# A fourteenth seven-product pair in each half of a down projection, and three kept sums reused across the halves

## Chip, core and metric

The kernel runs on one core of a Trainium2 chip. The metric is device time in microseconds; the median of three runs before the change is 1292.85 us (1292.70 to 1292.91). The engines are TensorE (PE; its weight loads are PEld), VectorE (DVE), ScalarE (ACT), GpSimd (POOL) and SyncE (SP). In this kernel SP issues the loads of weights, and POOL issues, in this stage, the reads of sums that were kept in DRAM.

## What is computed

One layer of an encoder over 256 positions of width 2048, in float32. The change touches the last product, `act @ w_down`, with an inner dimension of 5504 = 43 x 128.

```
def conv_ffn(x, g_norm, w_up, conv_k, conv_b, w_down):
    h = rms_norm(x, g_norm)
    up = h @ w_up
    ...
    gate, val = jnp.split(up, 2, axis=-1)
    return x + (jax.nn.silu(gate) * val) @ w_down
```

A final RMSNorm follows. Everything before (a mixer block with two branches, an output projection, the up projection) is as it was.

## The kernel before

**Precision.** Each float32 operand is kept as a high and a low part, and a product is three matmuls (`triple`, L315 to L320: high by high, low by high, high by low). ScalarE makes the high part of a weight piece (L171), VectorE the low part by a subtraction (L172).

**Tiling of the down projection.** The 2048 output columns are done in two halves of 1024 (`g_dn`, two `wide` groups run by `run_wide`). Within a half the 43 inner chunks come as 21 pairs and a single one. A *piece* is one chunk's weights, 128 x 1024, 512 KB, so a half has pieces 0 to 42, and the second half's follow on. The pair that comes q-th is said to stand at *place* q; its pieces are 2q and 2q + 1.

**Two kinds of pairs.** A plain pair takes 2 pieces x 4 result blocks x 3 = 24 matmuls. A seven-product pair uses Winograd's form of the 2 x 2 block product (positions 2 x 128, chunks 2, columns 2 x 512): seven block products of three matmuls, 21 in all. Its first step (piece 2q) has three products, nine matmuls: blocks of the activations by blocks of both pieces' weights, the third with a sum of activations; its second step (piece 2q + 1) has four, twelve matmuls, with sums of weights in the order u13, u13, u24, u24. It accumulates in four banks P beside the four of the result, C. `ev_sums` adds the P banks into the result after the last such pair (a first half of five VectorE operations, L993 to L998, a second of three), `ev_down` and `finish` evict C.

**The sums.** The activation sums of each seven-product pair are made in the up projection (`sums`, `sums_split` in `ev_up`; four operations on 128 x 128 blocks and a split) and written to DRAM; in the down projection `stored` reads them back on POOL's queue, 512 KB, into one of three tiles s0, s1, s2 in turn, in both halves. The weight sums are of two kinds. For most pairs they are made on the spot: four VectorE additions of 128 x 512 (`weight_sums`, L361 to L365) in tiles t13 and t24, then split by ScalarE (L375) and VectorE (L376) into h13, l13, h24, l24, one tile each. For the pairs of DOWN_SPLIT (6, 10, 14, 18) they are made in the up projection (`split_ahead`), kept in DRAM as down_h and down_l, and read by `split_read` (four reads of 512 KB on POOL) into another set of tiles, one each. In a seven-product pair the first piece is split in its first half only; for a pair of DOWN_SPLIT only that half is loaded.

**Order.** The order of instructions on each engine is that of the program, written by hand. `begin(i)` precedes piece i's matmuls: it issues loads up to piece i + 4, splits piece i + 3, then runs the tasks listed for i, in the order in which they were listed. `wide` lists its tasks when the work is planned: for a pair whose first piece is i, the read of its activation sums at i - 4, weight sums at i - 3, their split at i - 2; for a pair of DOWN_SPLIT all reads at i - 6. Others are listed while the program runs: the convolution, gate and split of an up group at 1, 2 and 3 pieces behind its end (L1066 evicts it, L1072 to L1079 convolve), `ev_sums` at 1 and 2 behind the last seven-product pair. Raw weights have five buffers (`wraw`), split ones four (`whi`, `wlo`).

`down_order` lays the kept pairs (DOWN_PAIRS) on the places of DOWN_QUADS[g] and the others, in rising order, on the places left. The last four pieces of the second half are done block by block.

Of the kernel before, what the change touches and what calls it, by code (L numbers as in the profile page):

```python
# [25 lines left out]
NF = DFF // 128  # L26
# [42 lines left out]
TURN_X2 = (13, 1)  # L69
Y_GAP = 224  # L70
PAD = 16
DOWN_PAIRS = (3, 5, 6, 7, 9, 10, 11, 13, 14, 15, 17, 18, 19)
DOWN_QUADS = (DOWN_PAIRS, (2, 4, 5, 6, 8, 9, 10, 12, 13, 14, 16, 17, 18))
DOWN_SPLIT = (6, 10, 14, 18)
DOWN_JOBS = ((1, 3), (5, 7), (9, 11), (13, 17))
FIN_AT = 36
# [3 lines left out]
def trunk_kernel(ctx, tc, x, x_t, vecs, w_in, ln_g, ln_b, w_st, b_s, rpb, w_branch, w_out, w_up, w_down,  # L80
# [204 lines left out]
    def wide(src, row0, order, c0, acts, quads, room, done, sums=None, stored=None, split=None, late=False, lead=4, behind=()):  # L285
        n0 = plan_wide(src, row0, order, c0)
        boxes = {}
        for q in quads:
            i = n0 + 2 * q
            k = order[2 * q]  # L290
            units[i], units[i + 1] = 1, 2
            b = boxes[q] = {}
            ready = split[0].get(k // 2) if split else None
            if stored:
                b["acts"] = {}
                at(i - (ready[0] if ready else lead), lambda b=b, k=k: stored(k // 2, b["acts"]))
            else:
                b["acts"] = sums[k]
            if ready:
                halved.add(i)  # L300
                for n, lead in zip(("13", "24"), ready[-2:]):
                    at(i - lead, lambda b=b, k=k, n=n: split[1](k // 2, b, n))
                continue
            whole[i] = whole[i + 1] = None
            halves = late and q == quads[0]
            at(i - 3, lambda i=i, b=b, halves=halves: weight_sums(i, b, room, halves))
            if halves:
                at(i - 2, lambda b=b: b.pop("rest")())
            at(i - (1 if q in behind else 2), lambda b=b: weight_sums_split(b, room))
        return ("wide", n0, order, acts, quads, boxes, done)  # L310
# [41 lines left out]
    def sums_of(o):  # L352
        return [(o[:, 0, n * 128:(n + 1) * 128], o[:, 1, n * 128:(n + 1) * 128]) for n in range(4)]
# [629 lines left out]
    def ev_sums(j, room):  # L983
        def done(P, i):
            x2 = rs["x2"]
            p1, p5, p6, p7 = P
            x11, x12, x21, x22 = (x2[:, t, c * 512:(c + 1) * 512] for t in range(2) for c in (j, j + 1))
            m = {}

            def first_half():  # L990
                ab, cd = room("t13", F32), room("t24", F32)
                m["v"], m["u3"], m["w"] = cd[:, 0], cd[:, 1], ab[:, 0]
                nc.scalar.activation(ab[:, 0], p1, AF.Copy)  # L993
                nc.vector.tensor_add(x11, p1, x11)
                nc.vector.tensor_sub(ab[:, 1], ab[:, 0], p6)
                nc.vector.tensor_add(m["v"], p5, ab[:, 1])
                nc.vector.tensor_add(m["u3"], p7, ab[:, 1])
                nc.vector.tensor_add(m["w"], p5, m["u3"])  # L998

            def second_half():  # L1000
                nc.vector.tensor_sub(x12, x12, m["v"])
                nc.vector.tensor_add(x21, x21, m["u3"])
                nc.vector.tensor_sub(x22, x22, m["w"])

            at(i + 1, first_half)
            at(i + 2, second_half)
        return done
# [243 lines left out]
    def split_read(kept, g, tile_of, queue=nc.gpsimd):  # L1251
        def read(pair, box, n):
            u = box.setdefault("u", [])
            u.append([tile_of(pair, p + n) for p in "hl"])
            for t, src in zip(u[-1], kept[pair, g][n]):
                queue.dma_start(t.bitcast(F32), src)
            if len(u) == 2:
                split_sums(box, u)
        return read
# [130 lines left out]
    def down_room(name, dt):  # L1390
        return hpool.tile([128, 2, 512], dt, name=h_room[name])

    def stored(pair, box):
        n = ff["turn"] = (ff.get("turn", -1) + 1) % 3
        o = ff["twice"].tile([128, 2, 512], F32R, name="s2") if n == 2 else down_room(f"s{n}", F32R)
        nc.gpsimd.dma_start(o.bitcast(F32), ff["kept"][pair])
        box["s"] = sums_of(o)

    def down_split_tile(pair, name):
        return ff["twice"].tile([128, 2, 512], F32R, name=name)  # L1400
# [1 line left out]
    d_kept = {}  # L1402

    def down_order(g):
        free = [p for p in range(NF // 2) if p not in DOWN_PAIRS]
        kept = list(DOWN_PAIRS)
        pairs = [(kept if q in DOWN_QUADS[g] else free).pop(0) for q in range(NF // 2)]
        return tuple(2 * p + kk for p in pairs for kk in range(2)) + (NF - 1,)

    g_dn = [wide(w_d, 0, down_order(g), g * 1024, lambda k: ff["a"][k], DOWN_QUADS[g], down_room,  # L1410
                 (ev_sums(2 * g, down_room), ev_down if g == 0 else finish), stored=stored,
                 split=({p: (6, 6) for p in DOWN_SPLIT}, split_read(d_kept, g, down_split_tile))) for g in range(2)]
    ff["kept"] = {p: dram.tile([128, 2, 512], F32, name=f"sums{p}") for p in DOWN_PAIRS}
    for p, turn in zip(DOWN_SPLIT, DOWN_JOBS):
# [184 lines left out]
```

## Time and profile before

| | us |
|---|---|
| median of three runs | 1292.85 |
| profiled execution | 1293.06 |
| its span, first to last instruction | 1291.3 |
| down projection within the span | 1066.1 to 1283.2 |

The granted TensorE clock of this execution is 0.998. Rows of the profile are read so: a row of grouped instructions has line, engine, operation, output and inputs, shapes, count, then busy time and mean duration, then the idle time ahead of them and what ended it. A row of the timeline has start, duration, engine, line, operation and tiles; a run of equal instructions is one row with its count; the idle time of the engine ahead of it, and what ended that, stand in brackets. A row of waits has who waited for whom, the total in us, how often, and the longest. A row of a window has its limits, its length, and each engine's busy time (number of instructions), clock, share of the DMA engines and GB/s; asked for VectorE alone it has that engine's only. A row of DMA issues has the number, the size and the median us from issue to landing. A matmul's row overlaps the next one's, so that distances between starts count, not durations.

### The profile page before, as it was taken

To read this page: it belongs to the slowest core of one execution; us is meant where nothing else is said; L and a number is where in the kernel's file an instruction comes from. 1 tells how busy PE (TensorE), PEld (TensorE's weight loads), DVE (VectorE), ACT (ScalarE), POOL (GpSimd) and SP (SyncE) were. 2 spreads that over 40 slices of the span, in tenths; PEclk is the share of its full clock that TensorE was granted. 3 is DMA by queue.
4 is the path that set the end of the run, shared out by engine and by line. 5 is a ranking of instruction groups with operands and counts; after the bars stand their busy time and mean duration, and the time that the engine had idled before them with its cause. 6 is when DMAs were issued, how large, how long until landed. Compare 5 with 4: busy or idle time off the path is not lost.

```text
span 1291.3 us, 19690 instructions
## 1 busy us (share of the span) xinstructions
PE 1281.6 (99%) x6653; PEld 1092.7 (85%) x6653; DVE 1143.6 (89%) x1712; ACT 815.7 (63%) x1229; POOL 174.5 (14%) x309
## 2 busy tenths in 40 slices
PE   9999999999999999999999999999999999999997
PEld 7888888888888888888888888888888888888885
DVE  7898978888889988996888899998988989989987
ACT  7776577877855655566566656566665656555554
POOL 0003706334000001100001001100000001211210
PEclk9999999999999999999999999999999999999999
DMA  9779879998799977965588788888877859998993
GB/s 368 273 272 282 289 236 306 322 316 300 275 335 349 353 244 244 412 225 164 182 295 274 239 297 290 270 267 285 266 220 222 279 171 363 368 388 325 353 383 146
DMA packets 199893, 369.51 MB, mean 286 GB/s; under 512 B 15984, under 2 KB 124144, under 8 KB 199792
## 3 DMA queue, kind: packets, MB, share of 16 engines
q1 hardware_dynamic: 175472, 286.36, 64.6%
q0 software_dynamic: 23888, 81.23, 17.8%
q8 instruction: 52, 0.85, 0.3%
q10 hardware_dynamic: 432, 0.66, 0.1%
q14 instruction: 49, 0.40, 0.1%
HBM read 320.48 MB, written 45.61 MB: 284 GB/s over the span
## 4 chain that ended last, share of the span: by engine, by line
PE 98%; DVE 1%; issue 0%; DVEq 0%; ACT 0%; ACTq 0%
PE bank L223 31%; PE bank L227 16%; PE bank L320 12%; PE bank L318 12%; PE bank L319 12%; PE bank L251 5%; PE bank L253 5%; PE bank L252 5%; PE bank L835 1%; DVE wlo L172 0%; PE bank L885 0%; PE bank L499 0%; PE bank L699 0%; PE bank L875 0%; PE bank L973 0%
## 5 line engine op out<-in xcount | busy, mean ns | idle before, releaser
L172 DVE TENSOR_TENSOR wlo<-wraw,whi 128x1024 fp32r<-128x1024 f32 (+1 forms) x472 | 537.0, 1151 | 98.2 <-ACT whi L171 64.2
L171 ACT ACTIVATE whi<-wraw 128x1024 fp32r<-128x1024 f32 (+1 forms) x472 | 463.3, 995 | 187.9 <-PE bank L319 72.4
L223 PE MATMUL bank<-h,whi 128*128 128x512 f32 x1760 | 425.5, 392 | 0.0
L223 PEld LDWEIGHTS bank<-h,whi 128*128 128x128 f32 x1760 | 322.0, 188 | 61.8
L227 PEld LDWEIGHTS bank<-h,wlo 128*128 128x128 f32 x1760 | 225.9, 191 | 8.8
L227 PE MATMUL bank<-h,wlo 128*128 128x256 f32 x1760 | 228.6, 283 | 0.0
L1074 ACT ACTIVATE tc<-ta,ck 128x256 f32<-128x256 f32 x86 | 47.1, 595 | 110.0 <-DVE ta L1072 110.0
L320 PE MATMUL bank<-wlo,a 128*128 128x512 f32 x188 | 73.4, 390 | 0.2 <-DVE wlo L172 0.2
L318 PE MATMUL bank<-whi,h 128*128 128x512 f32 x186 | 73.2, 394 | 0.0
L318 PE MATMUL bank<-whi,a 128*128 128x512 f32 x188 | 73.2, 389 | 0.0
L319 PE MATMUL bank<-whi,a 128*128 128x512 f32 x188 | 73.1, 389 | 0.0
L319 PE MATMUL bank<-whi,h 128*128 128x512 f32 x186 | 72.8, 391 | 0.0
L320 PE MATMUL bank<-wlo,h 128*128 128x512 f32 x186 | 72.6, 390 | 0.0
L1077 DVE SCALAR_TENSOR_TENSOR tc<-ta,ck,tc 128x255 f32<-128x255 f32 x86 | 41.4, 481 | 14.4 <-ACT tc L1074 14.4
L800 POOL TENSOR_SCALAR_AFFINE_SELECT bias<-run 64x128 f32<-64x128 f32 x64 | 39.7, 654 | 85.4 <-DVE sc L843 84.7
L1306 POOL DMA_DIRECT2D down_h<-so x16 | 8.7, 545 | 311.1 <-ACT tc L1084 170.3
L251 PE MATMUL bank<-whi,y 128*128 128x512 f32 x128 | 50.6, 395 | 0.0
L251 PE MATMUL bank<-whi,h 128*128 128x512 f32 x128 | 50.4, 394 | 0.0
L253 PE MATMUL bank<-wlo,h 128*128 128x512 f32 x128 | 49.9, 390 | 0.0
L253 PE MATMUL bank<-wlo,y 128*128 128x512 f32 x128 | 49.9, 390 | 0.0
L252 PE MATMUL bank<-whi,y 128*128 128x512 f32 x128 | 49.8, 389 | 0.0
L252 PE MATMUL bank<-whi,h 128*128 128x512 f32 x128 | 49.8, 389 | 0.0
(332 smaller groups left out, 2075.7 us busy)
## 6 DMA issues: line engine op xcount, KB each, us to landing
wraw<-in_w_up_dram SPq DMA_DIRECT2D x336, 256.0 KB, 4.0
wraw<-in_w_in_dram SPq DMA_DIRECT2D x107, 512.0 KB, 6.3
wraw<-in_w_down_dram SPq DMA_DIRECT2D x78, 512.0 KB, 7.3
wraw<-in_w_in_dram SPq DMA_DIRECT2D x70, 256.0 KB, 6.0
wraw<-in_w_branch_dram SPq DMA_DIRECT2D x32, 512.0 KB, 5.7
wraw<-in_w_out_dram SPq DMA_DIRECT2D x28, 512.0 KB, 6.1
h<-sums POOLq DMA_DIRECT2D x18, 512.0 KB, 7.6
tw<-in_w_down_dram POOLq DMA_DIRECT2D x8, 1024.0 KB, 8.3
```

The costliest lines, as they stand in the source:

```text
L171: nc.scalar.activation(h[:, k, :m], w[:, k, :m], AF.Copy)
L172: nc.vector.tensor_sub(l[:, k, :m], w[:, k, :m], h[:, k, :m].bitcast(F32))
L223: nc.tensor.matmul(p, h[:, k - k0, b * 128:(b + 1) * 128], acts(k), start=k == 0, stop=k == nk - 1)
L227: nc.tensor.matmul(p[:, :T], l[:, k - k0, b * 128:(b + 1) * 128], acts(k)[:, 0, :], start=False, stop=False)
L251: nc.tensor.matmul(p, xh, h[:, kk, :m], start=st, stop=False)
L252: nc.tensor.matmul(p, xl, h[:, kk, :m], start=False, stop=False)
L253: nc.tensor.matmul(p, xh, l[:, kk, :m], start=False, stop=sp)
L318: nc.tensor.matmul(p, xh, h, start=st, stop=False, **kw)
L319: nc.tensor.matmul(p, xl, h, start=False, stop=False, **kw)
L320: nc.tensor.matmul(p, xh, l, start=False, stop=sp, **kw)
L1074: nc.scalar.activation(v, u, AF.Identity, scale=ck[:, 1, ch:ch + 1], bias=ck[:, 3, ch:ch + 1])
L1077: nc.vector.scalar_tensor_tensor(v[:, 1:], u[:, :T - 1], ck[:, 0, ch:ch + 1], v[:, 1:], op0=OP.mult, op1=OP.add)
```

## The change

DOWN_PAIRS becomes the union of two lists, DOWN_KEPT, one for each half, which now also fix the order of the kept pairs. Both lists hold the thirteen pairs of before and pair 2, so each half has 14 seven-product pairs and 7 plain ones, and pair 2's sums are kept too. `stored` remembers which pair stands in which of the three tiles and reads nothing if the pair is already there; the last three kept pairs of the first half (17, 18, 19) are the first three of the second.

Places and kept pairs (an s marks a pair of DOWN_SPLIT, with weight sums from DRAM):

| half | before: pair at place | after: pair at place |
|---|---|---|
| first | 3 at 3; 5, 6s, 7 at 5 to 7; 9, 10s, 11 at 9 to 11; 13, 14s, 15 at 13 to 15; 17, 18s, 19 at 17 to 19 | 2 at 2; 3, 6s, 5 at 4 to 6; 7, 10s, 9 at 8 to 10; 11, 13 at 12, 13; 14s, 15, 17, 18s, 19 at 15 to 19 |
| second | 3 at 2; 5, 6s, 7 at 4 to 6; 9, 10s, 11 at 8 to 10; 13, 14s, 15 at 12 to 14; 17, 18s, 19 at 16 to 18 | 17, 18s, 19 at 1 to 3; 2, 6s, 3 at 5 to 7; 5, 10s, 7 at 9 to 11; 9, 11 at 13, 14; 14s, 13, 15 at 16 to 18 |

```diff
-DOWN_PAIRS = (3, 5, 6, 7, 9, 10, 11, 13, 14, 15, 17, 18, 19)
-DOWN_QUADS = (DOWN_PAIRS, (2, 4, 5, 6, 8, 9, 10, 12, 13, 14, 16, 17, 18))
+DOWN_KEPT = ((2, 3, 6, 5, 7, 10, 9, 11, 13, 14, 15, 17, 18, 19), (17, 18, 19, 2, 6, 3, 5, 10, 7, 9, 11, 14, 13, 15))
+DOWN_PAIRS = tuple(sorted(set(DOWN_KEPT[0] + DOWN_KEPT[1])))
+DOWN_QUADS = ((2, 4, 5, 6, 8, 9, 10, 12, 13, 15, 16, 17, 18, 19), (1, 2, 3, 5, 6, 7, 9, 10, 11, 13, 14, 16, 17, 18))
...
+    down_held = {}
+
     def stored(pair, box):
+        held = [s for p, s in down_held.values() if p == pair]
+        if held:
+            box["s"] = held[0]
+            return
         n = ff["turn"] = (ff.get("turn", -1) + 1) % 3
         o = ff["twice"].tile([128, 2, 512], F32R, name="s2") if n == 2 else down_room(f"s{n}", F32R)
         nc.gpsimd.dma_start(o.bitcast(F32), ff["kept"][pair])
         box["s"] = sums_of(o)
+        down_held[n] = pair, box["s"]
...
     def down_order(g):
-        free = [p for p in range(NF // 2) if p not in DOWN_PAIRS]
-        kept = list(DOWN_PAIRS)
+        free = [p for p in range(NF // 2) if p not in DOWN_KEPT[g]]
+        kept = list(DOWN_KEPT[g])
```

## The prediction

> **What bounds the kernel now.** I read the page first, then the waits of TensorE, then the busy time of the stage that the change touches, the down projection, which runs from 1066.1 us to 1283.2 us of the span.
>
> ```profile
> span 1291.3 us, 19690 instructions
> PE 1281.6 (99%) x6653; PEld 1092.7 (85%) x6653; DVE 1143.6 (89%) x1712; ACT 815.7 (63%) x1229; POOL 174.5 (14%) x309
> PE 98%; DVE 1%; issue 0%; DVEq 0%; ACT 0%; ACTq 0%
> ```
>
> TensorE has no free time, and the chain of work that ended last is 98% TensorE. In the window from 1060 us to the end, its waits by the profile are one line, and VectorE is nearly as full:
>
> ```profile
> PE bank L320 <- DVE wlo L172: 0.2, 1, 0.2
> ...
> 1066.10:1283.20 217.10, 198.09 (x250) 1.00 0.89 335
> ...
> 400.00:800.00 400.00, 400.00 (x2078) 343.39 (x2077) 357.12 (x540) 241.56 (x348) 25.79 (x45) 1.00 0.80 273
> ```
>
> So a matmul removed is time saved only while VectorE (198.09 of 217.10 us busy here, 19.0 idle) and the transfers still deliver each operand in time. Where they are just in time today, anything put ahead of them is a stall of TensorE, and stalls cannot be won back, since nothing behind them is idle.
>
> **The matmuls removed.** A plain pair is 24 matmuls, a seven-product pair 21; one pair changes kind in each half, so six go.
>
> ```profile
> 1077.17 0.39 PE L318 MATMUL bank<-whi,a 128*128 128x512 f32 x1
> 1078.31 0.39 PE L320 MATMUL bank<-wlo,a 128*128 128x512 f32 x1
> ...
> 1273.92 0.39 PE L319 MATMUL bank<-whi,a 128*128 128x512 f32 x1
> 1274.54 0.50 PE L320 MATMUL bank<-wlo,a 128*128 128x512 f32 x1 [0.23 <-DVE wlo L172]
> ```
>
> 1077.17 is the first matmul of piece 4 of the first half; by the loops the one at 1273.92 is the 868th after it, so one matmul takes 196.75 / 868 = 0.227 us. Six are 1.36 us; a plain pair is 5.45 us, a seven-product pair 4.77 us (its first step 2.04, its second 2.72). **Term 1: -1.36 us.**
>
> **The opening of the first half.** The first seven-product pair moves from place 3 (piece 6) to place 2 (piece 4), while VectorE still does the convolution of the last up group.
>
> ```profile
> 1071.67 2.35 DVE L172 TENSOR_TENSOR wlo<-wraw,whi 128x1024 fp32r<-128x1024 f32 x2
> 1073.94 0.75 DVE L1072 TENSOR_TENSOR ta<-ta,rb 128x256 f32<-128x256 f32 x2
> ...
> 1076.86 1.22 DVE L172 TENSOR_TENSOR wlo<-wraw,whi 128x1024 fp32r<-128x1024 f32 x1
> ...
> 1078.33 0.68 DVE L172 TENSOR_TENSOR wlo<-wraw,whi 128x512 fp32r<-128x512 f32 x1
> 1078.93 0.68 DVE L364 TENSOR_TENSOR h<-wraw 128x512 f32<-128x512 f32 x1
> ...
> 1081.46 0.42 DVE L543 TENSOR_TENSOR a<-tc,a 128x256 fp32r<-128x256 f32 x1
> ```
>
> The first row splits pieces 3 and 4 (2.27 us from start to next start, 1.135 each), the convolution takes 1073.94 to 1076.86 = 2.92, then piece 5 is split. A half split costs 0.60 (1078.33 to 1078.93), the four weight sums 2.53 (1078.93 to 1081.46). In the changed kernel begin(1) splits half of piece 4 and then makes the weight sums of pieces 4 and 5; that task was listed when the work was planned, the convolution only when its group ended, so the sums go first; the rows 1078.93 to 1081.46 show that order, as L543 too was listed late and stands behind the sums of the same begin. Piece 5's split starts at 1071.67 + 1.135 + 0.60 + 2.53 + 2.92 = 1078.86 and ends 1.22 later, 1080.08. TensorE needs its low half in the sixth matmul of the pair, which is where the row 1078.31 stands; with the 0.05 us that the wait at 1274.54 shows behind the end of its split (1273.27 + 1.22, below) it goes on at 1080.13. Nothing covers this: VectorE is busy all the way. **Term 2: +1.8 us** (1.5 to 2.1). The sums' own splits follow at 1081.2 and 1082.4, before TensorE, now late, wants them (1081.5 and 1082.9).
>
> **The read of pair 18 in the first half.** Pairs 6, 10, 14 and 18 get their weight sums from DRAM, into one set of tiles. From pair 14 to pair 18 there were four places (14 to 18), one pair between them plain; now there are three (15 to 18), all seven-product.
>
> ```profile
> 1243.55 0.39 PE L320 MATMUL bank<-l,h 128*128 128x512 f32 x1
> ...
> 1244.24 0.53 POOL L1396 DMA_DIRECT2D h<-sums  x1 [4.22 <-PE bank L320]
> ...
> 1246.32 0.53 POOL L1256 DMA_DIRECT2D l<-down_l  x1
> ...
> l<-down_l POOLq DMA_DIRECT2D x1, 512.0 KB, 13.0
> ...
> l<-down_l POOLq DMA_DIRECT2D x1, 512.0 KB, 15.2
> ...
> DMA to landing us min/median/max: 7.6/11.5/15.2
> ```
>
> Five reads leave in a row once the earlier pair's sums have been used: 0.69 us after the ninth matmul of its second step began (1243.55 to 1244.24), the fifth 2.08 us after the first. So the fifth leaves 8 x 0.227 + 0.69 + 2.08 = 4.59 us after that second step began. It is needed in the ninth matmul of pair 18's second step. From second step to second step there lie 12 + 21 + 21 + 9 = 63 matmuls, 14.30 us; with 1.82 that is 16.12, so the read has 11.5 us, against 17.0 before. Issue to landing of the fifth read took 13.0 us and 15.2 in the two bursts shown, and 15.2 is the longest of all sixteen l reads: 1.5 to 3.7 too long. Against that, the new order holds VectorE up just there (next term), so fewer weight loads share the transfer engines with the burst; by that the stall could be nothing. **Term 3: +0.9 us**, between nothing and the nearest row's 1.5, closer to the row; ends 0 and 3.7. For this queue the Trainium skill ("DMA: Bandwidth & Descriptors", Anatomy of one DMA) fits 2.0 us plus bytes / 436 GB/s; five reads of 512 KB would by my estimate from it be down in about 8 us, term 3 would be nothing and the sum +1.5. The rows of 13.0 and 15.2 disagree with that where the weights' queue runs too; the same page (Queues, rings and completion order) has the transfer engines take turns between queues, and by my estimate its 6 us of data doubled, and 2.0, give 14.
>
> **Two computed pairs in a row.** Before, a pair with sums from DRAM or a plain one stood between any two whose sums are made here. Now places 12 and 13, 16 and 17 of the first half, 13 and 14, 17 and 18 of the second hold such pairs in a row, and their split sums (h13, l13, h24, l24) have one tile each. ScalarE can write h24 of the second only after the last matmul of the first.
>
> ```profile
> 1097.35 0.39 PE L320 MATMUL bank<-h,a 128*128 128x512 f32 x1
> 1097.76 1.06 ACT L375 ACTIVATE h<-h 128x1024 fp32r<-128x1024 f32 x1 [0.24 <-PE bank L320]
> 1263.22 2.35 DVE L376 TENSOR_TENSOR h<-h,h 128x1024 fp32r<-128x1024 f32 x2
> 1264.17 0.39 PE L318 MATMUL bank<-whi,a 128*128 128x512 f32 x1
> 1265.49 4.62 DVE L172 TENSOR_TENSOR wlo<-wraw,whi 128x1024 fp32r<-128x1024 f32 x4
> 1270.03 0.68 DVE L994 TENSOR_TENSOR x<-bank,x 128x512 f32<-128x512 f32 x1
> ...
> 1273.27 1.22 DVE L172 TENSOR_TENSOR wlo<-wraw,whi 128x1024 fp32r<-128x1024 f32 x1
> ```
>
> ScalarE starts 0.41 us after that matmul's start (1097.35 to 1097.76), so 0.18 after the second pair's first; it takes 1.06, VectorE's l24 another 1.135: l24 is done 2.4 us into the second pair, and is needed 2.04 + 8 x 0.227 = 3.9 us into it. That holds at three of the four, and the pieces split behind it are in time by about 1 us. The fourth is the last pair of the second half, and behind it VectorE has no slack. Today pair 18's matmuls there begin at 1264.17 and VectorE is through the sums' split at 1265.49, 1.32 us later; then come four splits, the first sums of the result (1270.03 to 1273.27) and the split of the last piece, whose product ran at 1274.54 instead of 1273.92 + 0.227 = 1274.15. That chain has no gap. With 2.4 in place of 1.32 it moves 1.1 us later and TensorE with it. **Term 4: +1.1 us** (0.7 to 1.4).
>
> **What is covered.** Pair 2's kept sums add four small and one 128x512 operation on VectorE in the up projection, some 1.8 us by the next rows, plus a write of 512 KB. They fall in the fourth up group, inside 400 to 800 us, where TensorE shows 400.00 of 400.00 us while pairs 6 and 10 already do the same beside such a job: nothing, and at most those 1.8 us.
>
> ```profile
> 1050.66 0.28 DVE L324 TENSOR_TENSOR sw<-tc 128x128 f32<-128x128 f32 x1
> ...
> 1053.91 0.68 DVE L543 TENSOR_TENSOR so<-sw,so 128x512 fp32r<-128x512 f32 x1
> ```
>
> Pair 2's read becomes the first of POOL's queue in this stage, and pair 3's follows.
>
> ```profile
> 1065.63 0.54 POOL L1396 DMA_DIRECT2D h<-sums  x1 [9.95 <-PE bank L227]
> 1066.56 0.54 POOL L1396 DMA_DIRECT2D h<-sums  x1 [0.40 <-PE bank L223]
> ...
> h<-sums POOLq DMA_DIRECT2D x18, 512.0 KB, 7.6
> ```
>
> They leave when the tiles of the up projection are free, at 1065.63 and 1066.56, and 7.6 us later, at 1073.2 and 1074.2, are there; the first is needed at 1077.17 + 6 x 0.227 = 1078.5. Nothing. The reads of kept sums go from 26 to 25 (14 + 11), since pairs 17, 18 and 19 stay in their tiles; no read before was waited for by TensorE, so this gives no time. VectorE's work grows, per half, by 0.60 + 1.135 + 2.53 + 2.27 less a plain pair's 2.27, 4.3 us, so 8.5 of its 19.0 idle us.
>
> **The sum.** -1.36 + 1.8 + 0.9 + 1.1 = +2.4. On the profiled execution (1293.06 us: the span 1291.3 and 1.76 around it) that is 1295.5; the median, 1292.85, lies 0.2 lower, so 1295.3.
>
> **Rivals.** *A, not slower: the opening is covered.* If piece 5 is split ahead of the convolution and the sums, VectorE is done with it by 1076.0 and term 2 is gone. It decides in one place: whether that split ends before 1078.3. Then -1.36 + 1.1 + 0 to 0.9: 1292.6 to 1293.5. For it: ScalarE, which makes the high half first, is busy 63% of the span. Against it: VectorE's order in the rows from 1071.67 on, which has no gap.
>
> *B, clearly slower: VectorE runs out across the two halves.* From the split of piece 32 to that of the second half's piece 3 it has the pairs 15, 17 and 19 at 6.54 us (0.60 + 1.135 + 2.53 + 2.27), 1.74 for pair 18, five plain pieces at 1.135, the result's sums at 3.24 (1270.03 to 1273.27) and 1.81 (1171.65 to 1173.46), the four evictions at 2.4, and 0.60 + 2.53 + 1.135 for pair 17 of the second half.
>
> ```profile
> 1171.65 0.68 DVE L1001 TENSOR_TENSOR x<-x,h 128x512 f32<-128x512 f32 x1
> ...
> 1173.46 1.22 DVE L172 TENSOR_TENSOR wlo<-wraw,whi 128x1024 fp32r<-128x1024 f32 x1
> 1174.60 2.47 DVE L1112 TENSOR_TENSOR x<-bank,x 128x512 f32<-128x512 f32 x4
> ...
> DVE h L365 <- DMA wraw<-in_w_down_dram: 3.5, 6, 1.2
> ```
>
> That is 38.8 us. TensorE's 182 matmuls from piece 29 to where that last split is needed take 41.3, and about 0.8 pass before the first split can start (0.18 and ScalarE's half split): 1.7 to spare, less some 0.7 for the wait for tiles at place 17. Late weights cost VectorE 3.5 us in six waits today, up to 1.2 each; more than one of those here makes a stall. With 1 to 3 us from this or from term 3 at its far end the time is 1296.5 to 1298.5. For it: the transfer engines are 89% busy over the stage. Against: term 3's own stall gives VectorE time.
>
> *C, the reuse doesn't act* and pairs 17, 18 and 19 are read again. Each read takes 7.6 us and would leave when its tile is free, two or more places ahead of its use; TensorE waits for none of this kind today, so this is within 0.3 us of the forecast.
>
> **Chances.** Forecast 0.60 (1293.7 to 1296.5: the terms' bounds, term 3 up to 1.5), A 0.17, B 0.20, C 0.03. A measurement of this kernel can tell about 0.2%, 2.6 us, from no change: up to 1295.4. Of the forecast and C a little over half lie below that, all of B above: slower 0.50, same 0.48. Faster by 0.2% would need 2.6 us; all that six matmuls and the 0.4 at 1274.54 hold is 1.8, so 0.02. The range takes A's upper part and B's lower: 1293.0 to 1298.2.
>
> **What would show it.** TensorE's count falls by 6; L364 runs 20 times in the stage, not 18; 25 reads of sums. Term 2: a wait of L320 on L172 of 1.8 us near 1078. Term 3: a wait on the reads of down_l or down_h near 1162. Term 4: the wait near 1275 grows from 0.2 to about 1.3. The forecast is wrong if TensorE's waits in the stage sum to under 2 us or to more than 6, or if a wait stands at the second half's first pairs.

## The result, and the profile after

| | before | after |
|---|---|---|
| median, us | 1292.82 (6 runs, 1292.70 to 1293.39) | 1296.53 (6 runs, 1296.17 to 1300.08) |
| ratio to before | | 1.0034 [1.0024, 1.0045] |
| profiled execution, its span | 1293.06, 1291.3 | 1296.51, 1294.7 |
| first matmul of the down projection to the end of the span | 225.15 | 228.80 |

The changed kernel is 3.7 us slower, and 3.65 us of that lie between the first matmul of the down projection and the end. These are the page's lines on the whole execution:

```profile
span 1294.7 us, 19696 instructions
PE 1281.3 (99%) x6647; PEld 1090.7 (84%) x6647; DVE 1153.4 (89%) x1729; ACT 817.6 (63%) x1234; POOL 175.0 (14%) x309
PE 96%; DVE 1%; DMA 1%; issue 0%; ACT 0%; POOL 0%; DVEq 0%; ACTq 0%; POOLq 0%
```

TensorE has six instructions fewer, as it should, and the chain that ended last is 96% TensorE where it was 98%: a transfer (DMA) has come onto it with 1%, and VectorE's share is 1% as before. The groups of VectorE's instructions and the DMA issues, both from 1060 us on, show that the rest of the change acts as written:

```profile
L365 DVE TENSOR_TENSOR h<-wraw 128x512 f32<-128x512 f32 x20 | 13.7, 683 | 0.0
```

```profile
h<-sums POOLq DMA_DIRECT2D x17, 512.0 KB, 7.7
...
s<-sums POOLq DMA_DIRECT2D x8, 512.0 KB, 7.6
```

20 weight sums of this form, not 18, and 17 + 8 = 25 reads of kept sums, so the reuse is real. VectorE's busy time from the first matmul of the stage to the place in the work that 1283.2 marked before (its window has limits, length, VectorE, clock, DMA share, GB/s):

```profile
1065.90:1286.65 220.75, 206.87 (x262) 1.00 0.86 327
```

It is 8.8 us busier (198.09 before) and has 13.9 us idle left of 19.0. The waits of TensorE's matmuls in the window from 1060 us on were one line of 0.2 us. Now they are:

```profile
PE bank L321 <- DVE wlo L173: 2.5, 3, 1.2
PE bank L321 <- DMA l<-down_l: 1.0, 1, 1.0
PE bank L319 <- ACT whi L172: 0.5, 1, 0.5
```

Five waits in four places. What each costs is read from the starts of matmuls: 0.227 us is the distance of two that run on, the rest is loss. Each wait is followed by one more distance that is 0.11 too long; it is counted with its wait.

| place | before | after |
|---|---|---|
| opening of the first half, 1078 to 1080 | 0 | 1.94 |
| reads of pair 18's weight sums, 1162.8 (and 0.11 at 1165.6, behind the next read of kept sums) | 0 | 1.35 |
| crossing into the second half, 1184.1 | 0 | 0.65 |
| last pair of the second half, 1278.0 | 0.50 | 1.44 |
| elsewhere (1069) | 0.11 | 0.11 |

The waits grew by 4.88 us, six matmuls less save 1.36: +3.52 of the measured +3.65. The first place, in TensorE's timeline and then in VectorE's (before, pieces 4 and 5 were split by 1078.1 and no matmul there waited):

```profile
1078.28 0.50 PE L319 MATMUL bank<-whi,a 128*128 128x512 f32 x1 [0.47 <-ACT whi L172]
1078.62 0.40 PE L320 MATMUL bank<-whi,a 128*128 128x512 f32 x1
1079.93 0.50 PE L321 MATMUL bank<-wlo,a 128*128 128x512 f32 x1 [0.92 <-DVE wlo L173]
```

```profile
1073.21 0.68 DVE L365 TENSOR_TENSOR h<-wraw 128x512 f32<-128x512 f32 x1
...
1075.74 0.75 DVE L1073 TENSOR_TENSOR ta<-ta,rb 128x256 f32<-128x256 f32 x2
...
1078.26 0.48 DVE L1080 SCALAR_TENSOR_TENSOR tc<-ta,ck,tc 128x255 f32<-128x255 f32 x1
1078.66 1.22 DVE L173 TENSOR_TENSOR wlo<-wraw,whi 128x1024 fp32r<-128x1024 f32 x1
```

The weight sums (from 1073.21), the convolution (1075.74 to 1078.66) and only then the split of piece 5, 0.2 us from the 1078.86 that was foretold. There are two waits, not one: the first is for ScalarE's high half of the same piece. The other three places stand in the chain of work that ended last (start, duration, what):

```profile
1148.07 0.55 POOL h L1403
...
1150.23 12.53 DMA l<-down_l
1162.80 0.50 PE bank L321
...
1182.60 0.27 DVE x L1113
1182.87 1.14 DVE wlo L173
1184.06 0.50 PE bank L321
...
1276.74 1.22 DVE wlo L173
1278.00 0.50 PE bank L321
```

POOL issues its five reads from 1148.07; the fifth leaves at 1150.23 and takes 12.53 us, and TensorE stands until it lands. At 1184 and 1278 TensorE waits for VectorE's split. Behind the wait at 1184 stand weights that came late to ScalarE, and behind ScalarE to VectorE:

```profile
1166.30 1.06 ACT L172 ACTIVATE whi<-wraw 128x1024 fp32r<-128x1024 f32 x1 [1.50 <-PE bank L321]
1168.85 1.06 ACT L172 ACTIVATE whi<-wraw 128x1024 fp32r<-128x1024 f32 x1 [1.49 <-DMA wraw<-in_w_down_dram]
```

```profile
1167.39 1.23 DVE L173 TENSOR_TENSOR wlo<-wraw,whi 128x1024 fp32r<-128x1024 f32 x1 [1.33 <-ACT whi L172]
1169.94 1.23 DVE L173 TENSOR_TENSOR wlo<-wraw,whi 128x1024 fp32r<-128x1024 f32 x1 [1.32 <-ACT whi L172]
```

The piece at 1168.85 waited for its load. For the one at 1166.30 the view names a matmul that ended at about the same time, but this piece's load landed only at 1166.20, 9.04 us after its issue, and that alone would have held it. VectorE lost 1.33 and 1.32 us behind these two pieces, and from 1169.94 to the split at 1182.79 it has no gap: the loss is carried for 13 us to the place where it is felt. At the last pair the rows of VectorE, and in the second fence of ScalarE, are:

```profile
1264.79 1.22 DVE L173 TENSOR_TENSOR wlo<-wraw,whi 128x1024 fp32r<-128x1024 f32 x1
1266.45 2.58 DVE L377 TENSOR_TENSOR h<-h,h 128x1024 fp32r<-128x1024 f32 x2 [0.45 <-ACT h L376]
1268.95 4.62 DVE L173 TENSOR_TENSOR wlo<-wraw,whi 128x1024 fp32r<-128x1024 f32 x4
```

```profile
1265.36 1.06 ACT L376 ACTIVATE h<-h 128x1024 fp32r<-128x1024 f32 x1 [3.56 <-PE bank L320]
1266.72 1.06 ACT L376 ACTIVATE h<-h 128x1024 fp32r<-128x1024 f32 x1 [0.30 <-PE bank L320]
```

The split of the sums waits for ScalarE, and ScalarE for the tiles that the pair before still uses (both its rows wait for TensorE). It is done 2.25 us into the pair (1266.70 to 1268.95; 1.32 before).

### The profile page after: what moved, and what is told of

The parts are those of the page before. It is cut to its first block, busy times and chain, and to the rows that moved or that the text cites. A ratio compares the mean times of both kernels' runs of the same rounds, so it can differ in the third digit from the quotient of the medians.

```text
span 1294.7 us, 19696 instructions
## 1 busy us (share of the span) xinstructions
PE 1281.3 (99%) x6647; PEld 1090.7 (84%) x6647; DVE 1153.4 (89%) x1729; ACT 817.6 (63%) x1234; POOL 175.0 (14%) x309
## 4 chain that ended last, share of the span: by engine, by line
PE 96%; DVE 1%; DMA 1%; issue 0%; ACT 0%; POOL 0%; DVEq 0%; ACTq 0%; POOLq 0%
PE bank L224 31%; PE bank L228 16%; PE bank L321 11%; PE bank L319 11%; PE bank L320 11%; PE bank L252 5%; PE bank L254 5%; PE bank L253 4%; DMA l<-down_l 1%; DVE wlo L173 1%; PE bank L836 1%; PE bank L886 0%; PE bank L500 0%; PE bank L700 0%; PE bank L1049 0%
## 5 line engine op out<-in xcount | busy, mean ns | idle before, releaser
L1075 ACT ACTIVATE tc<-ta,ck 128x256 f32<-128x256 f32 x86 | 47.1, 595 | 112.0 <-DVE ta L1073 112.0
L321 PE MATMUL bank<-wlo,a 128*128 128x512 f32 x176 | 68.9, 392 | 2.5 <-DVE wlo L173 2.5
L319 PE MATMUL bank<-whi,a 128*128 128x512 f32 x176 | 68.6, 390 | 0.5 <-ACT whi L172 0.5
L320 PE MATMUL bank<-whi,a 128*128 128x512 f32 x176 | 68.5, 389 | 0.0
L376 ACT ACTIVATE h<-h 128x1024 fp32r<-128x1024 f32 x40 | 42.0, 1058 | 26.0 <-PE bank L320 12.9
```

The source lines that it names most:

```text
L319: nc.tensor.matmul(p, xh, h, start=st, stop=False, **kw)
L320: nc.tensor.matmul(p, xl, h, start=False, stop=False, **kw)
L321: nc.tensor.matmul(p, xh, l, start=False, stop=sp, **kw)
L376: nc.scalar.activation(h, t, AF.Copy)
L1075: nc.scalar.activation(v, u, AF.Identity, scale=ck[:, 1, ch:ch + 1], bias=ck[:, 3, ch:ch + 1])
```

## The experiments

Twelve kernels, e1 to e12. Where a distance between matmuls is given, it is the loss beyond 0.227 us as above; "the stage" is first matmul of the down projection to the end of the span (225.15 before, 228.80 after). Medians are given against the kernel before, run again beside each experiment. In the diffs, `...` and the words before and after stand for parts that are as in "The change".

**The parts alone.** The change has three: a fourteenth pair in the first half, one in the second, and the reuse. First, in e1, the reuse with thirteen pairs in both halves:

```diff
 DOWN_KEPT = (
-  (2, 3, 6, 5, 7, 10, 9, 11, 13, 14, 15, 17, 18, 19), (17, 18, 19, 2, 6, 3, 5, 10, 7, 9, 11, 14, 13, 15))
+  (3, 5, 6, 7, 9, 10, 11, 13, 14, 15, 17, 18, 19), (17, 18, 19, 3, 6, 5, 7, 10, 9, 11, 13, 14, 15))
 DOWN_QUADS = (
-  ..., (1, 2, 3, 5, 6, 7, 9, 10, 11, 13, 14, 16, 17, 18))
+  (as before), (2, 3, 4, 6, 7, 8, 10, 11, 12, 14, 16, 17, 18))
```

> Thirteen kept pairs in both halves as before; the first half as before, the second opens at places 2 to 4 with pairs 17, 18, 19 left in their tiles. The same 21- and 24-matmul pairs as before, three reads of sums fewer. Lateness theory (the change's loss is four separate late operands): nothing is late that was not, so 1292.5 to 1293.3 us, TensorE's waits in the stage 0.2 to 0.9 us. Rival (the reuse itself, which puts pair 17's weight sums ahead of the evictions of the first half, costs the 0.6 us seen near 1184): about 1293.5.

1292.84 against 1292.79, ratio 1.0002 [0.9992, 1.0011]; the stage 225.33, all of the +0.18 in the last wait (0.69 for 0.50). Reads that nothing waited for give nothing when they are left out, and pairs 17 to 19 near the head of the second half (places 2 to 4 here) cost nothing by themselves.

Then, in e2, the first half changed, the second as before:

```diff
-DOWN_KEPT, DOWN_QUADS = (after, after), (after, after)
+DOWN_KEPT, DOWN_QUADS = (after, before), (after, before)
```

> The first half as after the change (14 pairs), the second as before (13, no reuse). Lateness theory: -0.7 for three matmuls, the opening wait of 1.9 near 1078 and the wait of 1.2 on the read of down_l near 1162 both stay, no wait near 1184, the last wait near 1275 back at 0.4: together +2.4, 1295.2 us. Rival (VectorE's added work of 4.3 us a half is what costs, wherever it lies): half of the change's loss, 1294.7 us, with waits spread over the half.

1296.01, ratio 1.0029 [1.0017, 1.0041], the stage 228.08 (+2.93): the opening 1.94 as in the whole change, the reads 1.86 and 0.25 more just behind, no wait at the crossing and none at the end. VectorE loses 1.25 and 1.40 us to two late pieces here too (1167.52 and 1170.14), but the second half of before has no weight sums to make at that place, and the loss isn't felt. And, in e3, the second half changed, the first as before:

```diff
-DOWN_KEPT, DOWN_QUADS = (after, after), (after, after)
+DOWN_KEPT, DOWN_QUADS = (before, after), (before, after)
```

> The first half as before (13 pairs), the second as after the change (14, with reuse). Lateness theory: -0.7 for three matmuls, no wait near 1078 or 1162, the last wait near 1275 at 1.3 to 1.4 (+1.0), the wait at the second half's opening between nothing and 0.65: 1293.1 to 1293.8 us. Rival (VectorE's added work costs wherever it lies): 1294.7 us.

1293.80, ratio 1.0009 [0.9999, 1.0018], the stage +0.33. The waits of TensorE in this kernel, from 1060 us on, are one line:

```profile
PE bank L321 <- DVE wlo L173: 1.2, 1, 1.2
```

It is the last pair's, 1.45 for the 0.50 of before; -0.68 + 0.95 = +0.27. So the first half bears the loss, the second about breaks even, and the wait at 1184 needs both, the late weights of the first and pair 17 at place 1 of the second: it is in neither run.

**The opening.** If VectorE's convolution is what stands ahead of piece 5, leaving out its taps for the last up group (e4) must take the wait down by their length:

```diff
-                for u, v, ch in c:
+                for u, v, ch in c if f0 + 1 < NF else ():
```

> The kernel after the change, without the two outer taps of the convolution for the last 128 channels of gate and of value (four VectorE operations of 0.48 us at 1076.8 to 1078.7 left out, so that part of the result is other). Lateness theory: VectorE reaches the split of piece 5 at 1076.8 instead of 1078.7, the two opening waits (0.7 and 1.2) fall to 0.2 or less in all, the others stay: 1294.7 us, 1.8 below the kernel after. Rival (piece 5's load or ScalarE is late): the opening wait stays over 1 us and the time within 0.5 of the kernel after.

It did not. 1296.48, ratio 1.0033 [1.002, 1.0046]; the two waits fell from 0.63 and 1.09 to 0.63 and 0.70. VectorE's row and, in the second fence, ScalarE's of this kernel:

```profile
1076.23 0.76 DVE L1073 TENSOR_TENSOR ta<-ta,rb 128x256 f32<-128x256 f32 x2
1078.76 1.23 DVE L173 TENSOR_TENSOR wlo<-wraw,whi 128x1024 fp32r<-128x1024 f32 x1 [1.77 <-ACT whi L172]
```

```profile
1076.69 1.09 ACT L1075 ACTIVATE tc<-ta,ck 128x256 f32<-128x256 f32 x2 [4.31 <-DVE ta L1073]
1077.69 1.04 ACT L172 ACTIVATE whi<-wraw 128x1024 fp32r<-128x1024 f32 x1
```

VectorE, freed, waits 1.77 us for ScalarE. ScalarE has two operations of the convolution (L1075) ahead of piece 5 and stood 4.31 us until VectorE had made their input, which VectorE makes behind the weight sums. Two engines that each run in order block each other, and the theory of VectorE's queue alone was half of it. The next kernel, e12, also leaves out the products (L1073), so that ScalarE waits for nothing there:

```diff
-                    nc.vector.tensor_mul(u, u, rs["rb"])
+                    if f0 + 1 < NF:
+                        nc.vector.tensor_mul(u, u, rs["rb"])
...
-                for u, v, ch in c:
+                for u, v, ch in c if f0 + 1 < NF else ():
```

> The kernel after, without VectorE's part of the convolution of the last 128 channels of gate and value (the products with the row scales and both outer taps, six operations; that part of the result is other), so that ScalarE's part waits for nothing either. Theory (piece 5 is late through both engines: its split stands behind ScalarE's two operations of that convolution, which wait for VectorE's products, and behind VectorE's taps): the waits near 1078 and 1080, 1.8 after the change and 1.5 without the taps alone, fall to 0.2 or less. Rival (piece 5's load or the weight sums): 1 or more is left.

```profile
1076.01 1.22 DVE L173 TENSOR_TENSOR wlo<-wraw,whi 128x1024 fp32r<-128x1024 f32 x1
```

Piece 5 is split by 1077.2, and the whole opening wait is gone: its cause is shown. Yet the time is 1297.75 (three runs, 1296.15 to 1298.08), ratio 1.0034 [1.0019, 1.0049]. In the profiled execution, the slowest of the three, the stage takes 230.12. The wait at the crossing (0.65) is gone as well, but the wait for the reads is 2.16 in place of 1.24, two new ones of 0.20 stand at 1247 and 1267, and the one at the end is 2.48 in place of 1.44, with a further loss behind it (last section). Why the end's wait grew stays open. For the reads the reason is in the trace: POOL issues them 1.64 us earlier than in the changed kernel (1146.43 and 1148.07), but the fifth lands 0.72 earlier (1162.03 and 1162.75), and 1.64 - 0.72 is the 0.92 by which the wait grew.

Leaving nothing out, the convolution was also moved one piece later (e5):

```diff
-            at(i + 1, lambda: conv(0))
+            at(i + (2 if f0 + 1 == NF else 1), lambda: conv(0))
```

> The kernel after, with the convolution of the last up group listed one piece later, so that it stands behind the split of piece 5 and behind the split of pair 2's weight sums on both VectorE and ScalarE; nothing is left out. Theory (that convolution, through ScalarE's order as much as VectorE's, is what makes piece 5 late): the waits near 1078 and 1080, 1.7 in all with 0.2 of restart, become one of 0.5 to 1.2 near 1082 at piece 6, whose split now stands behind the convolution; first matmul of the stage to the end of the span 227.7 to 228.3 us against 228.8. Rival (VectorE has too much to do before piece 6 whatever the order): 228.6 or more.

Median 1298.22 of 8 runs (1296.12 to 1298.82), ratio 1.0038 [1.0027, 1.0048]. In the profiled execution, 1296.12, the stage takes 228.23, within what was expected; the opening costs 1.27 at 1082 to 1084, the reads 0.60, the crossing 0.95, the end 1.45. The conflict moves with the convolution. The median shows no gain: five of the eight runs lie above 1298, which stays open, and the profiled one is the lowest.

**The reads and the crossing.** In the first half of e6 pair 14 goes back to place 14, so that four places lie between the two pairs with stored weight sums, and the plain pair moves to 15:

```diff
-DOWN_QUADS = ((2, 4, 5, 6, 8, 9, 10, 12, 13, 15, 16, 17, 18, 19), ...
+DOWN_QUADS = ((2, 4, 5, 6, 8, 9, 10, 12, 13, 14, 16, 17, 18, 19), ...
```

> The kernel after, with pair 14 of the first half at place 14 and the plain pair at place 15, so that pair 14 and pair 18 are four places apart again. Theory (the fifth read has 11.5 us where it takes 12.5 and more): the wait on down_l near 1162 is gone, the others stay: 227.5 us from the stage's first matmul to the end, against 228.8. Rival (given back: that stall gave VectorE time, which the crossing of the two halves now lacks): the wait near 1184 grows from 0.65 to 1.3 or more and the stage takes 228.2 or more.

1294.38, ratio 1.0011 [1.0001, 1.0021], the stage 226.70: 2.1 us won where only the 1.24 at 1162 had been expected to go. The waits of TensorE in this kernel:

```profile
PE bank L321 <- DVE wlo L173: 2.1, 2, 1.2
PE bank L319 <- ACT whi L172: 0.5, 1, 0.5
```

No line for down_l is left, and of the three waits for VectorE two: the opening and the end. The one at the crossing went with the reads'. The order of pairs 17 to 19 around the crossing is that of the change, so VectorE's work there is the same; what differs is that the first half's burst leaves 5.8 us earlier (1142.26 and 1148.07) and is down by 1157.9 before the second half's reads of pair 18 leave from 1161. In the changed kernel the two bursts join (fifth read down at 1162.75, the next issued at 1161.44), and the weights beside them are the late ones shown above. So the one misplaced pair cost both waits, the second of them together with pair 17 at place 1 (above).

**The end.** In e7 the last three pairs come in the order computed, stored, computed, so that no two computed ones are in a row there:

```diff
-DOWN_KEPT[1]: ..., 11, 14, 13, 15)
+DOWN_KEPT[1]: ..., 11, 13, 14, 15)
```

> The kernel after, with the last three seven-product pairs of the second half in the order 13, 14, 15: the pair whose weight sums come from DRAM stands between the two whose sums are made here. VectorE's and TensorE's work are the same. Theory (ScalarE can write h24 of the last pair only after the last matmul of the pair before): the wait near 1278 falls from 1.44 to 0.4 to 0.7, 227.9 us from the stage's first matmul to the end against 228.8. Rival (VectorE's work since the last plain pair makes it late): the wait stays at 1.2 or more.

A miss: 1296.78, ratio 1.0033 [1.0023, 1.0044]; the last wait is still 1.26. ScalarE's rows of this kernel:

```profile
1258.31 1.06 ACT L172 ACTIVATE whi<-wraw 128x1024 fp32r<-128x1024 f32 x1 [1.89 <-DMA wraw<-in_w_down_dram]
1260.85 0.63 ACT L172 ACTIVATE whi<-wraw 128x512 fp32r<-128x512 f32 x1 [1.48 <-DMA wraw<-in_w_down_dram]
1263.30 1.06 ACT L172 ACTIVATE whi<-wraw 128x1024 fp32r<-128x1024 f32 x1 [1.82 <-DMA wraw<-in_w_down_dram]
```

Now the weights are late. Pair 14's four reads stand on POOL behind a read of sums whose tile is still in use, leave from 1247.09 to 1248.65, the last landing at 1262.81, and the weights beside them take up to 9.74 us. The order alone trades one cause for another.

To size the tile's release by itself, the last pair of the changed kernel got, in e11, other tiles for its split sums (those of the stored kind, free by then):

```diff
+    def ff_split(name, dt):
+        return ff["twice"].tile([128, 2, 512], dt, name=name)
...
+            into = ff_split if src is w_d and c0 and q == quads[-1] else room
-            at(i - (1 if q in behind else 2), lambda b=b: weight_sums_split(b, room))
+            at(i - (1 if q in behind else 2), lambda b=b, into=into: weight_sums_split(b, into))
```

> The kernel after, order 14, 13, 15 kept, but the last pair of the second half splits its weight sums into the tiles that pair 14 has done with (the set for sums from DRAM) instead of those that the pair before still holds. Nothing else is changed. Theory (ScalarE waits for that tile until the pair before is done, and VectorE's last chain starts that much late): VectorE has no idle time before the split of those sums, which ends 0.7 earlier, and the wait near 1278 falls from 1.44 to about 0.7. Rival (the tile is not what is late): the wait stays at 1.3 or more.

```profile
1264.80 1.22 DVE L173 TENSOR_TENSOR wlo<-wraw,whi 128x1024 fp32r<-128x1024 f32 x1
1265.94 2.36 DVE L381 TENSOR_TENSOR l<-h,h 128x1024 fp32r<-128x1024 f32 x2
1268.21 4.62 DVE L173 TENSOR_TENSOR wlo<-wraw,whi 128x1024 fp32r<-128x1024 f32 x4
```

VectorE runs without a gap, 0.74 us earlier than in the changed kernel (1268.21 and 1268.95), and the last wait is 0.69: the release is 0.75 of the 1.44. For the rest VectorE is busy without a gap from 1255.11 on; 0.50 stood there before the change too, and that two computed pairs in a row make up what is left is argued, not shown. The runs show none of the gain: 1296.38, ratio 1.0033 [1.0021, 1.0044], where the spread alone is 1295.0 to 1299.75.

**Towards a better kernel.** In e8 the first half is as before, the second as changed with the order 13, 14, 15 at the end:

```diff
-DOWN_KEPT, DOWN_QUADS = (after, after), (after, after)
+DOWN_KEPT, DOWN_QUADS = (before, after with 13, 14, 15 last), (before, after)
```

> The first half as before (13 pairs), the second with 14 pairs and reuse as after, with its last three in the order 13, 14, 15. Theory: three matmuls less and no new wait: 224.5 us from the stage's first matmul to the end against 225.15 before and 225.5 with the order 14, 13, 15; 1292.1 to 1292.5 us. Rival (the second half's waits are of VectorE's load): 225.4 or more, 1293.0 or more.

1292.24 against 1293.16, ratio 0.9993 [0.9983, 1.0003]: the median is as expected and no longer slower, but the profiled execution (1293.22) has a stage of 225.70, on the rival's side, with 1.49 at the end, and its chain there holds a load of weights of 9.18 us. So in e9 pair 14's four reads of weight sums are listed earlier, 8 pieces ahead and so in front of the read of its own activation sums, on whose tile they had to wait:

```diff
-split=({p: (6, 6) for p in DOWN_SPLIT}, ...
+split=({p: (4, 8, 8) if (p, g) == (14, 1) else (6, 6) for p in DOWN_SPLIT}, ...
```

> As the run with the second half alone and its last three pairs in the order 13, 14, 15, but in the second half the four reads of pair 14's weight sums are listed two pieces earlier and ahead of the read of its activation sums, so that on POOL's queue they no longer stand behind a tile that the pair at place 13 holds. Theory (in that order the last wait is from weights that land late, because those four reads share the transfer engines with them near the end): the last wait falls to 0.5 or less in the profile as well, 224.4 to 224.7 us from the stage's first matmul to the end, 1291.9 to 1292.3 us. Rival (it is VectorE's load, not the weights): the last wait stays at 1.2 or more.

1291.73 (11 runs, 1291.27 to 1292.77) against 1292.68 (26 runs), ratio 0.9990 [0.9981, 0.9999]. One thing more is in the edit: the loop of `wide` that sets the 8 keeps it for the pairs behind (as it keeps the 6 elsewhere, so that the activation sums of computed pairs behind a stored one are read at i - 6, not i - 4). So the edit also puts the read of the last pair's activation sums ahead of pair 14's. Here the load that took 9.18 us takes 7.66, and the next two take 7.24 and 6.06 for 9.26 and 8.08. No matmul of the stage waits; all that the view lists from 1060 us on is a weight load:

```profile
PEld bank L321 <- DVE wlo L173: 0.3, 1, 0.3
```

The stage is 223.94, 1.21 less than before: three matmuls, 0.68, and the wait at the end, 0.50. This kernel is ahead of both, by about 0.1%, and its interval only just leaves out no difference. The same early reads in the whole change (e10):

```diff
-DOWN_KEPT[1]: ..., 11, 14, 13, 15)
+DOWN_KEPT[1]: ..., 11, 13, 14, 15)
-split=({p: (6, 6) for p in DOWN_SPLIT}, ...
+split=({p: (4, 8, 8) if (p, g) == (14, 1) else (6, 6) for p in DOWN_SPLIT}, ...
```

> The kernel after, with the order 13, 14, 15 at the end and with pair 14's reads early as in the run beside it. Theory (the kernel after has two causes of its last wait, each alone enough: the tile that the pair before still holds, and, where that is taken away by the order, late weights): the wait near 1278, 1.44 after the change and 1.26 with the order alone, falls to 0.3 to 0.7; the other waits stay. Rival (VectorE's load): 1.2 or more.

1295.86, ratio 1.0028 [1.0017, 1.0038]. The wait at the end is gone here too (1.44), but in the profiled execution a new one of 1.03 stands at 1248.8, and the stage is 228.43. Its origin lies 34 us ahead. ScalarE around 1212 us, in the changed kernel and then in this one, where the program up to there is the same:

```profile
1212.03 1.05 ACT L172 ACTIVATE whi<-wraw 128x1024 fp32r<-128x1024 f32 x1
1214.00 1.06 ACT L172 ACTIVATE whi<-wraw 128x1024 fp32r<-128x1024 f32 x1 [0.93 <-DMA wraw<-in_w_down_dram]
```

```profile
1211.87 1.04 ACT L172 ACTIVATE whi<-wraw 128x1024 fp32r<-128x1024 f32 x1
1215.04 1.06 ACT L172 ACTIVATE whi<-wraw 128x1024 fp32r<-128x1024 f32 x1 [2.12 <-DMA wraw<-in_w_down_dram]
```

Every instruction issues 0.26 us earlier here, yet this load lands 1.04 later (issued at 1206.14 and 1206.40, down at 1214.94 and 1213.90), the next ones too. VectorE falls behind by 1.9 us against TensorE between 1207 and 1218 and does not make it up: at 1249 it is still behind by as much, and there the pairs at places 13 and 14, both computed, need it.

## Why the prediction came out as it did

It said slower by 2.4 us, 1295.3, within 1293.0 to 1298.2; it is slower by 3.7, 1296.5. The place of three of the four losses, their causes and the sign held. The number is less good than it looks: 1296.53 lies at the very end of what the forecast's own terms allowed (1296.5), and the range holds it easily only because it took in part of rival B.

*Term 1, -1.36.* Six instructions fewer, and e3 and e9 add up with 0.68 for three of them.

*Term 2, +1.8 at the opening.* 1.94, 0.11 of it the slow step behind a second wait. The place (VectorE's split at 1078.66 for 1078.86) and the size held, the mechanism was told by half. ScalarE had been given as a reason for rival A, since it is busy 63% of the span; e4 shows it as bound as VectorE there. Share of busy time was the wrong view for an engine that runs in order: what counts is which instruction stands ahead. Rival A is refuted by the trace of the change.

*Term 3, +0.9 at the reads.* 1.35. The allowance of 11.5 us was right: the fifth read took 12.53, 1.03 over, and the wait is 1.13 and 0.11. It was mis-sized by taking a value between nothing and the nearer row's 1.5. The reason for going below the row, fewer weight loads beside the burst, did not hold: between the issue of its first read and the landing of its fifth, six weight loads were issued before the change (in the burst of 13.0) and six after it. The Trainium skill ("DMA: Bandwidth & Descriptors", Queues, rings and completion order) was read as two queues sharing in turn, 14 us by that estimate, and its fit for one DMA (Anatomy of one DMA) as 8. The 12.53 lies nearer the first.

*Term 4, +1.1 at the end.* 1.44 less 0.50, 0.94. The split of the sums was done 2.25 us into the pair where 2.4 had been worked out. e11 shows that 0.75 of the 1.44 is the tile, e7 that the order of pairs alone doesn't cure it, since late weights lie right behind; the prediction had named no such second bound there.

*Covered.* Pair 2's read: no wait of TensorE names it. The up projection: the stage begins at 1065.91 for 1066.10, so it is no longer than before. The reuse: nothing, as said (e1, ratio 1.0002). VectorE's added work: 8.5 worked out, 8.8 measured.

*What failed: the crossing, 0 in the forecast.* The prediction set a wait at the second half's first pairs as a sign against itself, and 0.65 stands there. Rival B had named the place and the mechanism: 1.7 us to spare, less 0.7, and more than one late piece makes a stall. Two came, 1.33 and 1.32; 2.65 less 1.0 to spare less the 1.24 that the reads' wait gave VectorE leaves 0.4. The step that failed is having the two as alternatives: forecast and B were given separate chances, though what causes one (a burst of reads leaving later) is also part of the cause of the other, as e6 shows. And "term 3's own stall gives VectorE time", the reason against B, held only for half of what the burst cost.

By terms the forecast was off by +0.14, +0.45, -0.16 and +0.65, together 1.1 of the 1.25 between 2.4 and the 3.65 of the stage; 0.15 stays unassigned.

## What to carry to other kernels

When an engine is near full, cost a step that moves by the landing times of the transfers that move with it: a burst that leaves 5.8 us later made two waits 20 us apart, and taking it back won 2.1 us where the waiting read alone showed 1.24. Removing one wait is worth its length only if the transfers behind it have room, since earlier matmuls ask for the next reads earlier, and these need not land as much earlier (e12: of 1.94 won at the opening, 0.92 was lost again at the reads, which left 1.64 earlier and landed 0.72 earlier). For work shared by two engines in order, look at what stands ahead of the operand on both of them.

## What the hardware showed beside that

**Behind one wait of 2.2 us TensorE ran at about half its clock.** In the kernel without VectorE's part of the last convolution (e12) TensorE stood from 1275.8 to 1278.03. Its windows around that (limits, length, TensorE busy, granted clock, DMA share, GB/s):

```profile
1270.00:1278.10 8.10, 6.04 (x28) 1.00 0.01 4
1278.10:1280.00 1.90, 1.90 (x5) 0.52 0.00 0
1280.00:1283.00 3.00, 3.00 (x11) 0.74 0.00 0
```

For 3.4 us matmuls stand 0.43 us apart, about twice 0.227, which costs 1.7 us, 0.26 of it counted in the 2.48 above; then the clock is full again. A wait of 2.05 us at 1162 in the same execution did nothing of the kind (granted clock 1.00 behind it), and none of the shorter waits of the other kernels did. The Trainium skill ("TensorE: Matmul & The Clock Gate", Part 1: The HAM clock gate) has the clock fall after an idle window of about 3.4 us and return after a busy one of about 3.4 us. The return agrees; the fall came after 2.2 us, less than the page's window. It is one occurrence.

**The same loads landed up to 1.7 us apart in two executions.** With the same program up to there, 0.26 us apart, e10's execution had a load take 8.79 us and that of the changed kernel 7.50; the next took 10.11 and 8.34, the third 10.30 and 8.43. With VectorE 94% busy in the stage, this delay was carried for over 30 us. The runs of the crowded kernels also spread more (1296.17 to 1300.08 after, six runs) than those of the one in which nothing waits (1291.27 to 1292.77, eleven); that the landing times are the reason is likely by this, but wasn't tried.
